# Grouping TensorE matmuls by array shape in a two-layer RWKV-7 and latent-attention step

## The chip, the cores and the metric

The kernel runs on one core of one Trainium2 chip. The metric is the device time of one execution in microseconds (us). A change is told from no change by comparing the median of several runs.

## What is computed

One inference step of a two-layer decoder. Layer 0 mixes tokens by an RWKV-7 recurrence; layer 1 is multi-head latent attention over a latent key and value that come from the residual stream after layer 0. 16 meta tokens and 512 prompt tokens go through it, and 8 sequences of 4 new sample tokens each, which see 2048 past tokens in paged caches. Cut to the two parts that matter here, the reference is:

```python
def wkv7_scan(s0, r, decay, k, v, kk, ka):
    def step(s, inp):
        r_t, d_t, k_t, v_t, kk_t, ka_t = inp
        sa = jnp.einsum('bhvk,bhk->bhv', s, kk_t)
        s = s * d_t[:, :, None, :] - sa[..., None] * ka_t[:, :, None, :] + v_t[..., None] * k_t[:, :, None, :]
        return s, jnp.einsum('bhvk,bhk->bhv', s, r_t)
...
def mla_attend(q_lat, q_rope, q_pos, segments):
...
        for lat, kr, kp in segments:
            s = jnp.einsum('bhqr,bkr->bhqk', ql, lat) + jnp.einsum('bhqp,bkp->bhqk', qr, kr)
            s = s.astype(jnp.float32) * ATTN_SCALE
            scores.append(jnp.where(kp[None, None, None, :] <= qp[None, None, :, None], s, -jnp.inf))
        probs = jax.nn.softmax(jnp.concatenate(scores, axis=-1), axis=-1)
```

The state of a head is 64 x 64, there are 16 heads; attention has 8 heads with 128 plain and 64 rotary dimensions.

## The kernel before

**The recurrence.** The 560 tokens are handled in eight chunks of 64 prompt tokens and a ninth with the last 16 prompt tokens and the 32 sample tokens. Heads go in pairs: a pair's two heads lie on partitions 0 to 63 and 64 to 127 (`halves`, index `par`). Two groups of four pairs run one after the other (`chunks(0)`, then `chunks(1)`), and in a group two halves of two pairs each (`hf`) are stepped in turn, so that one's matmuls fill the other's waits. For one half of one chunk, `chunk` (line 898) does: `solve` (two products, L886 and L892, each followed by copies or scalings on ScalarE and VectorE: L888, L893, L894), the product for the new state (L905), whose result VectorE adds to the decayed state (L913, L915), and the **outputs**. For each of its four heads the outputs are two matmuls that add into one 64 x 64 place of a PSUM tile `q`: L920, in which all 128 partitions are summed over (array shape 128 rows x 64 columns), and L921, in which only the head's own 64 partitions are (64 x 64). Nothing in the recurrence waits for the outputs; ScalarE copies them to `Of` (L923). `tail` (line 966 and following) does the same for the ninth chunk, with L1006 and L1007 for eight heads. An fp32 matmul shows in the trace as two records.

Around it, other work is woven in by a table (`PLAN`): the inverses of the chunk matrices (`inverse`, many small steps on VectorE, L637 and L638; `merge`, with 32 x 32 matmuls L839 and L847, whose operands go through DRAM and are loaded by SP, L816 to L824), the late value projections (L326, with transposes L601), and for finished chunks the mixer's output (L1078 to L1096). The second group starts when its inverse and the values are done. The scheduler of the tile layer fixes each engine's order when the program is built.

**The scores.** In `mla`, `scores(h, i)` (line 1583) takes 128 queries of one head against their 144 to 528 keys, in one or two blocks of columns. Each block is a sum of five matmuls (L1594 to L1598); fp32 operands are split in a rounded high part and a low remainder. L1597 multiplies a tile `r`, which has the rotary queries' high part on one half of the partitions and the low part on the other, with `krh`, the high part of the rotary keys, which stands on both halves. L1598 multiplies only the high half of `r` (64 rows) with the low part `krl` of the keys. A last matmul adds the causal mask (L1599). Between the scores TensorE works on the sample tokens' attention over the paged cache (L1678, L1681, L1727), whose pages POOL and SP fetch.

Of the kernel before, what the change touches and what calls it, by code (L numbers as in the profile page):

```python
# [19 lines left out]
D = 1024  # L20
# [34 lines left out]
# ---------------------------------------------------------------- host layout  # L55
# [150 lines left out]
class Kern:  # L206
    NA, NB, NS, NM, NC = 21, 10, 9, 36, 22
# [44 lines left out]
    # ---- tiles  # L252
# [44 lines left out]
    # ---- weights  # L297
# [21 lines left out]
    def mm3(self, v, w, xs, off, n, first=True, last=True):  # L319
        """v: psum [128, 2, n]; w: (hi, lo) [128, kt, 128]; xs: per k-tile (hi, lo)"""  # L320
# [11 lines left out]
    def mmk(self, v, w, xs):  # L332
        """v: psum [128, n]; w: (hi, lo) [128, kt, 128]; xs: per k-tile (hi, lo), n wide"""
        wh, wl = w
        for k, (xh, xl) in enumerate(xs):
            for e, (wt, xt) in enumerate(((wh, xh), (wh, xl), (wl, xh))):
                self.nc.tensor.matmul(v, wt[:, k, :], xt, start=(k == 0 and e == 0), stop=(k == len(xs) - 1 and e == 2))  # L337
# [12 lines left out]
    def low(self):  # L350
        """what follows gives way to what the program has further on"""
# [33 lines left out]
    # ---- setup  # L385
# [23 lines left out]
    # ---- layer 0 mixing  # L409
    def rwkv(self):  # L410
# [23 lines left out]
        # normed input, its shift and the values, in two spans of tokens  # L434
# [134 lines left out]
        # low-rank paths  # L569
# [19 lines left out]
        # receptances; the values leave feature-major and, per chunk, token-major  # L589
# [32 lines left out]
        # inverses of the unit triangular chunk matrices, blocks of 32  # L622
# [47 lines left out]
        # heads in pairs: decay and rate (A), projection (B), chunk operands (C), scores (D)  # L670
# [127 lines left out]
        # recurrence over chunks, two groups of four pairs  # L798
# [98 lines left out]

        def chunk(st, c, hf):
# [19 lines left out]
            for i, pr, par in heads:  # L918
                o = q[halves[par], i * 64:i * 64 + 64]
                nc.tensor.matmul(o, V[:, pr, par, :], W[pr // 2][:, 2 * (pr % 2) + par, 64:128], start=True, stop=False)  # L920
                nc.tensor.matmul(o, Sp[halves[par], i, :], R[halves[par], pr, :], start=False, stop=True)  # L921
# [31 lines left out]
        # the sample tokens against their states, while the pair's operands are here  # L953
# [12 lines left out]
        def tail(st):  # L966
# [36 lines left out]
            for pr, par in heads:  # L1003
                hs = halves[par]
                o = q[hs, pr * 64:pr * 64 + 48]
                nc.tensor.matmul(o, V[:, pr, par, :], W[pr // 2][:, 2 * (pr % 2) + par, 64:112], start=True, stop=False)  # L1006
                nc.tensor.matmul(o, ident[hs, 64 * par:64 * par + 64], RS[hs, pr, 0:48], start=False, stop=True)  # L1007
# [54 lines left out]
        # output of the mixer, two pairs at a time, over columns a..b  # L1062
# [126 lines left out]
        # what is left, woven together: (steps, what must be through, after how many of its steps)  # L1189
# [42 lines left out]
    # ---- what follows an update of a tile of the residual stream  # L1232
    def begin(self, off, names):
        """norm statistics over columns off.. and split inputs with the gains names"""
# [20 lines left out]
    def stat(self, power):  # L1255
        """the mean square of post() to the given power, on all partitions"""
# [15 lines left out]
    def ffn_seg(self, q, a, b):  # L1272
        """a quarter of the hidden units for columns a..b"""
# [96 lines left out]
    # ---- latent attention  # L1370
    def mla(self):
        nc, tc, I, O, x = self.nc, self.tc, self.I, self.O, self.x
        ident = self.k["ident"]
        mp = self.mp
        mk = mp.tile([128, 320], BF16, name="mk")
# [52 lines left out]
        # down projections  # L1428
# [42 lines left out]
        # queries  # L1471
# [31 lines left out]
        # sample queries against the latent  # L1503
# [24 lines left out]
        # keys and values of the prompt, two heads at a time  # L1528
        KB = [(0, 16)] + [(16 + 128 * i, 128) for i in range(4)]
        kn, V, oo = [], [], [None] * NH  # L1530
        kh, kl = self.a("krh", dt=F32R), self.a("krl", dt=F32R)
        self.split(kh[:, :TP], kl[:, :TP], kr[:, :TP])
        zero = self.c("zero", [128, 512])
        nc.gpsimd.memset(zero, 0.0)
# [367 lines left out]
```

## Time and profile before

| | |
|---|---|
| median of 3 runs | 1768.58 us (1764.98 to 1772.23) |
| profiled execution, span from first to last instruction (the page gives no other time of it) | 1768.4 us |
| TensorE matmuls (PE) | 1653.7 us, 94% of the span |
| VectorE (DVE) | 970.6 us, 55% |
| ScalarE (ACT) | 665.8 us, 38% |
| GpSimd (POOL) | 349.0 us, 20% |
| mean granted TensorE clock | 0.937 |

Matmuls are pipelined, and the page models their ends, so busy shares of PE are no measure of how well it is used. What one matmul costs in a stream is read from the times at which neighbours start. The granted clock of a stretch is a mean: 1.00 is all of it at 2.4 GHz, 0.50 all of it at 1.2 GHz.

### The profile page before, as it was taken

The page shows a single profiled execution, that of the slowest core. Times are in us where ns is not written, and L with a number is a line of the kernel's source. Part 1 is how long each engine was busy: PE and PEld are TensorE (multiplying, and loading weights), DVE is VectorE, ACT ScalarE, POOL GpSimd, SP SyncE. Part 2 cuts the span into 40 slices and gives each one's busy share as a digit, 9 for nine tenths or more (in the row PEclk, how much of TensorE's full clock was granted, in tenths as well). Part 3 has the DMA queues.
Part 4 walks back from the last instruction along what each step waited for, and adds up shares of the span by engine and source line. Part 5 has one row for each costly group of instructions (what it writes and reads, how often), then busy time and mean ns, then how long its engine had stood idle before and what let it go on. Part 6 is the DMA issues. An engine that isn't in the chain of part 4 may idle for free.

```text
span 1768.4 us, 33338 instructions
## 1 busy us (share of the span) xinstructions
PE 1653.7 (94%) x13474; PEld 1494.1 (84%) x13474; DVE 970.6 (55%) x1600; ACT 665.8 (38%) x1232; POOL 349.0 (20%) x467
## 2 busy tenths in 40 slices
PE   7788878899999998899999999899999999999997
PEld 6577867777779887799999999766769999999996
DVE  6775696553426658665444565645635444444446
ACT  4374554322324433334333243244624332322222
POOL 4633435421100023200000010674420000000000
PEclk9899887796669999999999999999999999999999
DMA  6335647855623444444323243587622222322233
GB/s 211 111 101 150 189 145 202 254 173 133 191 92 100 156 157 154 144 153 148 113 85 97 84 134 106 174 254 230 211 85 92 86 86 84 93 87 84 86 93 99
DMA packets 156475, 240.04 MB, mean 136 GB/s; under 512 B 68417, under 2 KB 100082, under 8 KB 156322
## 3 DMA queue, kind: packets, MB, share of 16 engines
q1 hardware_dynamic: 140466, 189.59, 35.5%
q0 software_dynamic: 15280, 47.59, 8.3%
q8 instruction: 106, 1.74, 0.4%
q10 hardware_dynamic: 576, 0.74, 0.1%
q14 instruction: 47, 0.39, 0.1%
HBM read 200.50 MB, written 37.37 MB: 135 GB/s over the span
## 4 chain that ended last, share of the span: by engine, by line
PE 53%; ACT 1%; DVE 1%; issue 1%; DMA 1%; SPq 1%; POOL 0%; DVEq 0%; POOLq 0%; ACTq 0%
PE mm L326 30%; PE mm L337 12%; PE sm L337 2%; PE sm L1727 2%; PE sm L1634 1%; PE sm L1678 1%; PE mm L1598 1%; PE sm L1579 1%; PE sm L1618 1%; PE mm L1594 1%; ACT whi L307 0%; PE sm L1681 0%; DVE y L1839 0%; DVE wlo L308 0%; DMA lN<-latN,idx 0%
## 5 line engine op out<-in xcount | busy, mean ns | idle before, releaser
L307 ACT CAST whi<-raw 128x1024 fp32r<-128x1024 f32 x218 | 228.9, 1050 | 642.9 <-PE mm L326 357.9
L308 DVE TENSOR_TENSOR wlo<-raw,whi 128x1024 fp32r<-128x1024 f32 x214 | 266.7, 1247 | 279.2 <-ACT whi L307 276.9
L337 PE MATMUL mm<-xs,whi 128*128 128x256 f32 (+1 forms) x1024 | 200.7, 294 | 1.7 <-DVE fd L1299 0.9
L337 PEld LDWEIGHTS mm<-xs,whi 128*128 128x128 f32 x1024 | 163.3, 189 | 3.2 <-issue 1.4
L337 PE MATMUL mm<-xs,wlo 128*128 128x256 f32 (+1 forms) x512 | 149.7, 292 | 0.8 <-DVE wlo L308 0.8
L326 PE MATMUL mm<-hh,whi 128*128 128x272 f32 (+1 forms) x640 | 133.6, 290 | 0.0
L326 PE MATMUL mm<-hl,whi 128*128 128x272 f32 (+1 forms) x640 | 133.5, 290 | 0.0
L326 PE MATMUL mm<-hh,wlo 128*128 128x272 f32 (+1 forms) x640 | 133.5, 290 | 0.0
L326 PE MATMUL mm<-h_ffn,whi 128*128 128x272 f32 x512 | 106.2, 288 | 0.5 <-ACT fr L1333 0.5
L326 PE MATMUL mm<-h_ffn,wlo 128*128 128x272 f32 x512 | 106.3, 289 | 0.0
L326 PE MATMUL mm<-l_ffn,whi 128*128 128x272 f32 x512 | 105.8, 288 | 0.0
L326 PEld LDWEIGHTS mm<-hh,whi 128*128 128x128 f32 x640 | 100.9, 188 | 0.0
L326 PEld LDWEIGHTS mm<-hl,whi 128*128 128x128 f32 x640 | 100.9, 188 | 0.0
L326 PEld LDWEIGHTS mm<-hh,wlo 128*128 128x128 f32 x640 | 100.9, 189 | 0.0
L337 PEld LDWEIGHTS mm<-xs,wlo 128*128 128x128 f32 x512 | 96.8, 189 | 1.1 <-DVE wlo L308 1.0
L1837 POOL TENSOR_TENSOR y<-x,rstd 128x272 f32<-128x272 f32 x4 | 3.5, 891 | 459.5 <-ACT rstd L1831 459.5
L337 PE MATMUL mm<-hh,wlo 128*128 128x256 f32 (+1 forms) x256 | 77.0, 301 | 5.1 <-DVE wlo L308 5.1
L326 PEld LDWEIGHTS mm<-h_ffn,whi 128*128 128x128 f32 x512 | 80.8, 188 | 1.0 <-ACT fr L1333 1.0
L326 PEld LDWEIGHTS mm<-l_ffn,whi 128*128 128x128 f32 x512 | 80.3, 188 | 0.0
L326 PEld LDWEIGHTS mm<-h_ffn,wlo 128*128 128x128 f32 x512 | 80.0, 188 | 0.0
L337 PE MATMUL mm<-hl,whi 128*128 128x256 f32 (+1 forms) x256 | 76.7, 300 | 3.1 <-DVE hl L1291 3.0
L337 PE MATMUL mm<-hh,whi 128*128 128x256 f32 (+1 forms) x256 | 77.4, 302 | 0.1
(471 smaller groups left out, 3953.8 us busy)
## 6 DMA issues: line engine op xcount, KB each, us to landing
raw<-wall SPq DMA_DIRECT2D x222, 512.0 KB, 3.6
lT<-latT SPq DMA_DIRECT2D x80, 160.0 KB, 3.5
W_D<-sc POOLq DMA_DIRECT2D x16, 512.0 KB, 4.3
W<-W_D SPq DMA_DIRECT2D x32, 256.0 KB, 3.9
AK_D<-akt SPq DMA_DIRECT2D x8, 576.0 KB, 4.4
s<-state SPq DMA_DIRECT2D x16, 256.0 KB, 3.8
AKc<-AK_D SPq DMA_DIRECT2D x16, 256.0 KB, 4.0
V_D<-vt POOLq DMA_DIRECT2D x8, 288.0 KB, 3.5
```

Source lines behind the costliest of these rows:

```text
L307: nc.scalar.copy(hi, raw)
L308: self.lo_on.tensor_sub(lo, raw, hi.bitcast(F32))
L326: nc.tensor.matmul(v[:, h, :], wt[:, k, :], xt[:, off + h * n: off + (h + 1) * n], start=(first and k == 0 and e == 0), stop=(last and k = ...
L337: self.nc.tensor.matmul(v, wt[:, k, :], xt, start=(k == 0 and e == 0), stop=(k == len(xs) - 1 and e == 2))
L1579: nc.tensor.matmul(o, l[:, k0:k0 + kw], w[:, 2 + k, :], start=(k == 0 and e == 0), stop=(k == 1 and e == 2))
L1594: nc.tensor.matmul(o, qh[:, qs], nh[:, ks], start=True, stop=False)
L1598: nc.tensor.matmul(o, r[b, qs], kl[b, ks], start=False, stop=x < nb - 1)
L1618: nc.tensor.transpose(q[:, 128 * b:128 * b + 128], Pt[:, 16 + 128 * b:144 + 128 * b], ident)
L1634: nc.tensor.matmul(q[:, q0:], V[h // 2][b][:, 128 * (h % 2):128 * (h % 2) + 128], PT[b] if b else Pm[h % 2], start=(b == 0), stop=(b == 4))
L1678: nc.tensor.matmul(q[32 * bb:32 * bb + 32, cols], qlT[:, r, 4 * g + bb, :], lt[bb][:, :, 128 * r + 64 * k:128 * r + 64 * k + 64], start=(r ...
L1727: nc.tensor.matmul(qa[rs, 0:RANK], PT[jp // 2][:, o:o + 32], nat[bb][:, RANK * k:RANK * k + RANK], start=(jp == 0 and k == 0), stop=False)
L1837: nc.gpsimd.tensor_mul(y[:, i], x[m][:, s], r)
```

## The change

In `chunk` and `tail` the two output terms no longer alternate head by head. A helper takes the pairs in turn: for an even pair both heads' first term and then both heads' second, for an odd pair the other way round, so that neighbouring pairs meet in the same shape. In `mla` the low part of the rotary keys becomes two tiles of 128 rows, one with the keys on the upper half and zeros on the lower, one the other way; the fifth matmul of a score takes all 128 rows of `r`.

```diff
-    NA, NB, NS, NM, NC = 21, 10, 9, 36, 22
+    NA, NB, NS, NM, NC = 21, 10, 9, 37, 22
...
+        def alternate(inner, outer, prs):
+
+            for i, pr in enumerate(prs):
+                first, second = (outer, inner) if i % 2 else (inner, outer)
+                first(i, pr, True)
+                second(i, pr, False)
...
             q = self.sm()
-            for i, pr, par in heads:
-                o = q[halves[par], i * 64:i * 64 + 64]
-                nc.tensor.matmul(o, V[:, pr, par, :], W[pr // 2][:, 2 * (pr % 2) + par, 64:128], start=True, stop=False)
-                nc.tensor.matmul(o, Sp[halves[par], i, :], R[halves[par], pr, :], start=False, stop=True)
+
+            def inner(i, pr, first):
+                for par in range(2):
+                    nc.tensor.matmul(q[halves[par], i * 64:i * 64 + 64], V[:, pr, par, :], W[pr // 2][:, 2 * (pr % 2) + par, 64:128], start=first, stop=not first)
+
+            def outer(i, pr, first):
+                for par in range(2):
+                    nc.tensor.matmul(q[halves[par], i * 64:i * 64 + 64], Sp[halves[par], i, :], R[halves[par], pr, :], start=first, stop=not first)
+            alternate(inner, outer, [2 * hf, 2 * hf + 1])
...
-        kh, kl = self.a("krh", dt=F32R), self.a("krl", dt=F32R)
-        self.split(kh[:, :TP], kl[:, :TP], kr[:, :TP])
         zero = self.c("zero", [128, 512])
         nc.gpsimd.memset(zero, 0.0)
+        kh = self.a("krh", dt=F32R)
+        nc.scalar.copy(kh[:, :TP], kr[:, :TP])
+        kz = [self.a(f"krl{i}", dt=F32R) for i in range(2)]
+        for i, (a, b) in enumerate((halves, halves[::-1])):
+            nc.vector.tensor_sub(kz[i][a, :TP], kr[a, :TP], kh[a, :TP].bitcast(F32))
+            for c in (slice(0, TP // 2), slice(TP // 2, TP)):
+                nc.scalar.copy(kz[i][b, c], zero[b, :TP // 2])
...
-                nc.tensor.matmul(o, r[b, qs], kl[b, ks], start=False, stop=x < nb - 1)
+                nc.tensor.matmul(o, r[:, qs], kz[h % 2][:, ks], start=False, stop=x < nb - 1)
```

`tail` is changed like `chunk`, over `range(4)` pairs. In the built programs the orders of TensorE stand as follows.

TensorE in the recurrence of the first group, chunk 4, before: the end of a half's state product (`SUV`, `AKc`), its outputs, the rest of the other half's product, and the start of that half's outputs.

```order
L905 MATMUL sm<-SUV_4_3764,AKc_4_3765 64x64 x5
L920 MATMUL sm<-W_40_3762,SUV_4_3764 64x64
L921 MATMUL sm<-R_4_3766,Sp 64x64
L920 MATMUL sm<-W_40_3762,SUV_4_3764 64x64
L921 MATMUL sm<-R_4_3766,Sp 64x64
```

The same place in the change, both halves' outputs (L912, L928 and L932 are what L905, L920 and L921 were):

```order
L912 MATMUL sm<-SUV_4_3764,AKc_4_3765 64x64 x5
L928 MATMUL sm<-W_40_3762,SUV_4_3764 64x64 x2
L932 MATMUL sm<-R_4_3766,Sp 64x64 x4
L928 MATMUL sm<-W_40_3762,SUV_4_3764 64x64 x2
L912 MATMUL sm<-SUV_4_3764,AKc_4_3765 64x64 x3
L928 MATMUL sm<-W_41_3763,SUV_4_3764 64x64 x2
L932 MATMUL sm<-R_4_3766,Sp 64x64 x4
L928 MATMUL sm<-W_41_3763,SUV_4_3764 64x64 x2
```

Before, the pattern of two rows goes on to eight matmuls; now the same eight stand in three runs, and the run of the second term is four long. Over the whole program, neighbouring matmuls of different array shape number 733 before and 455 after.

ScalarE ahead of the first head's keys, in the change (`krl` are the two padded tiles, `knh` the first head's keys):

```order
L1552 CAST krh<-kr 128x528
L1557 CAST krl_11435<-zero 64x264 x2
L1557 CAST krl_11436<-zero 64x264 x2
L1561 CAST Vm_11443<-zero 80x256
L1561 CAST Vm_11444<-zero 80x256
L1561 CAST Pm_11445<-zero 80x512
L1561 CAST Pm_11446<-zero 80x512
L1572 CAST knh<-mm 128x528
```

The four casts of `krl` are new in this queue; the rest of it is as before. On TensorE the attention's scores and the sample's matmuls also change places in a few stretches. SP's queue moves in two places and POOL's in none.

## Rows read from the trace of the kernel before

**Rows 1.** The page, parts 1 and 2: busy time by engine, granted clock by slice.
```profile
PE 1653.7 (94%) x13474; PEld 1494.1 (84%) x13474; DVE 970.6 (55%) x1600; ACT 665.8 (38%) x1232; POOL 349.0 (20%) x467
...
PEclk9899887796669999999999999999999999999999
```

**Rows 2.** TensorE's waits from 345 to 535 us: total, times, longest.
```profile
PE mm L1085 <- ACT sqo L1081: 1.8, 1, 1.8
```

**Rows 3.** Windows, line 921 alone: PE and weight-load busy (records), clock, DMA share, GB/s.
```profile
345.00:394.00 49.00, 9.75 (x60) 5.63 (x60) 1.00 0.67 194
394.00:447.00 53.00, 13.74 (x68) 8.15 (x68) 0.60 0.48 128
447.00:490.00 43.00, 12.05 (x64) 7.09 (x64) 0.70 0.73 211
490.00:536.00 46.00, 9.28 (x49) 5.49 (x48) 0.71 0.26 78
560.00:590.00 30.00, 2.60 (x16) 1.50 (x16) 1.00 0.43 137
```

**Rows 4.** Timeline of TensorE from 353.9 us, high clock: start, length, line, shape, records.
```profile
353.97 0.69 PE L905 MATMUL sm<-SUV,AKc 128*64 128x64 f32 x16
354.49 0.28 PE L920 MATMUL sm<-W,SUV 128*64 128x64 f32 x2
...
356.49 0.40 PE L326 MATMUL mm<-xvl,whi 128*128 128x280 f32 x1
```

**Rows 5.** Timeline of TensorE, low clock: one call's outputs, first row and next work.
```profile
473.70 0.42 PE L920 MATMUL sm<-W,SUV 128*64 128x64 f32 x2
...
476.88 0.58 PE L905 MATMUL sm<-SUV,AKc 128*64 128x64 f32 x5
```

**Rows 6.** Timeline of TensorE, low clock: two runs in one shape.
```profile
470.67 1.12 PE L886 MATMUL sm<-SUV,W 128*64 128x64 f32 x16
471.79 1.12 PE L892 MATMUL sm<-rb,TT 64*64 64x64 f32 x16
```

**Rows 7.** Timeline of TensorE, high clock: a score with 400 keys.
```profile
1180.53 0.35 PE L1596 MATMUL mm<-knl,qnh 128*128 128x400 f32 x1
1180.72 0.34 PE L1597 MATMUL mm<-krh,qrs 128*128 128x400 f32 x1
1180.99 0.44 PE L1598 MATMUL mm<-krl,qrs 64*128 64x400 f32 x1
1181.37 0.23 PE L1599 MATMUL mm<-mk 128*128 128x128 bf16 x1
```

**Rows 8.** Timeline of ScalarE: the first casts from the zero tile.
```profile
1134.83 0.71 ACT L1538 CAST Vm<-zero 80x256 fp32r<-80x256 f32 x2 [8.64 <-POOL zero L1534]
```

**Rows 9.** Windows: busy PE, PEld, DVE, ACT, POOL (instructions), clock, DMA share, GB/s.
```profile
345.00:372.00 27.00, 27.00 (x265) 23.05 (x263) 22.90 (x64) 7.82 (x22) 9.45 (x14) 1.00 0.65 183
460.00:470.00 10.00, 9.78 (x111) 7.44 (x110) 5.37 (x17) 3.47 (x12) 1.67 (x4) 0.97 0.91 264
470.00:480.00 10.00, 10.00 (x83) 7.68 (x84) 1.74 (x6) 2.15 (x8) 0.85 (x3) 0.50 0.67 207
536.00:619.00 83.00, 81.39 (x650) 74.21 (x648) 53.43 (x96) 37.41 (x64) 8.16 (x16) 1.00 0.42 131
```

**Rows 10.** Timeline of SP's queue: the second group's inverse, first and last issues.
```profile
421.83 0.38 SPq L640 DMA_DIRECT2D X_D<-X  x1
...
430.25 8.50 SPq L824 DMA_DIRECT2D TT<-X_D  x14
```

**Rows 11.** DMA issues from 345 to 535 us: that load, KB each, us to landing.
```profile
TT<-X_D SPq DMA_DIRECT2D x16, 32.0 KB, 2.2
```

**Rows 12.** Timeline of TensorE: the last run that uses it.
```profile
443.73 1.91 PE L847 MATMUL sm<-TT,zs 32*32 32x32 f32 x62 [0.30 <-ACT zs L842]
```

**Rows 13.** Timeline of POOL: the second of twenty page gathers in a row.
```profile
1274.45 0.95 POOL L1720 DMA_INDIRECT lN<-latN,idx  x1 [0.30 <-issue]
```

**Rows 14.** Timeline of VectorE: the first half's next input.
```profile
473.93 0.61 DVE L913 TENSOR_TENSOR SUV<-sm,SL 64x128 f32<-64x128 f32 x2 [4.43 <-issue]
```

More of the change, by code (lines that the diff above doesn't have):

```diff
@@ L1002, in tail, with inner, outer @@
             q = self.sm()
[L1003 to L1007, printed above, removed]
+            def inner(i, pr, first):
+                for par in range(2):
+                    nc.tensor.matmul(q[halves[par], pr * 64:pr * 64 + 48], V[:, pr, par, :], W[pr // 2][:, 2 * (pr % 2) + par, 64:112], start=first, stop=not first)
+            def outer(i, pr, first):
+                for par in range(2):
+                    hs = halves[par]
+                    nc.tensor.matmul(q[hs, pr * 64:pr * 64 + 48], ident[hs, 64 * par:64 * par + 64], RS[hs, pr, 0:48], start=first, stop=not first)
+            alternate(inner, outer, range(4))
             for i in range(2):
@@ L1374, in mla @@
         mp = self.mp
+        halves = (slice(0, 64), slice(64, 128))
         mk = mp.tile([128, 320], BF16, name="mk")
@@ L1583, in scores @@
         def scores(h, i):
-            a, b = (slice(0, 128), slice(0, 64)) if h % 2 == 0 else (slice(0, 128), slice(64, 128))
             n = 16 + 128 * (i + 1)
```

## The prediction, made before the change was run

> **What bounds the kernel now.** I read the page first: TensorE (PE) is busy for 94% of the span, and the clock it was granted is at its high level except in a few slices early in the program [rows 1]. Those slices hold the recurrence over chunks, so I took the list of waits there next: in 190 us the longest line of TensorE's waits is 1.8 us [rows 2]. The time there is therefore TensorE's own, and the question is what it does with it. The two lines that the change rearranges run at 345 to 536 us and again at 577 to 590 us [rows 3]; 257 records of L921 were found, two to a matmul and eight to a call of `chunk`, so 32 calls. The granted clock of these windows is 1.00, 0.60, 0.70, 0.71 and 1.00. Of its two levels (1.2 and 2.4 GHz) a mean of 0.60 means a fifth of the time at the high one, so the records divide into 60 + 14 + 26 + 21 + 16 = 137 at the high level (53%) and 120 at the low one.
>
> The timeline shows where the time goes in one call. At the high level eight matmuls that alternate between 128x64 and 64x64 last from 354.49 to 356.49 us, 0.25 us each; just before, eight matmuls of L905, all 128x64, took 353.97 to 354.49, 0.065 each [rows 4]. At the low level the alternating eight last from 473.70 to 476.88, 0.40 us each [rows 5], and eight of L886 in one shape at most 1.12, of which 0.3 is the last one's own length and the wait for the copy behind it: about 0.11 each [rows 6]. **One change of shape thus costs about 0.185 us at the high level and 0.29 at the low one**, 0.234 as a mean over the 53 and 47 per cent.
>
> **The change, part by part.** In the built programs, neighbouring matmuls of different shape number 733 before and 455 after, 278 fewer.
>
> 1. Chunk outputs. Inside a call seven changes become two (5 x 32 = 160), and 18 calls more now end in the shape of what follows them, so 178 go. 178 x 0.234 = **41.7 us** of TensorE's time. Nothing else in the recurrence moves: the other engines' rows stand as they did, but for a few rows of VectorE's inverse.
> 2. Tails. Two calls of `tail`, together 20 changes fewer, one at each level: 10 x 0.29 + 10 x 0.185 = **4.7 us**.
> 3. Scores. With 400 keys, the matmul before the 64-row one starts 0.19 us after its neighbour, the 64-row one 0.27 after that, and the next 0.38 later [rows 7]. Three full-height ones would take 0.19 each: 0.08 + 0.19 = 0.27 us, and 40 such matmuls give **10.8 us**. A padded matmul streams the same columns, so it costs no more than its full-height neighbours.
> 4. What is added. Four ScalarE casts of zeros and one more VectorE subtract. ScalarE's zero casts before were two in 0.71 us and began when POOL's memset was done [rows 8]; four more stand behind the same memset and ahead of the first head's keys, which come 1.4 us later at most. The subtract falls where VectorE waits for TensorE anyway. The sample's scores cover it on TensorE; without them all of it would show. I charge 1 us (bounds 0 and 1.5).
>
> That is 57.2 - 1 = 56 us of TensorE's time at unchanged clocks. Not all of it can reach the end:
>
> - In the first chunks VectorE is busy 22.9 of 27 us [rows 9], so three calls gain little there: -2 (bounds 0 and -3.5).
> - The second group's recurrence needs its inverse, which goes through DRAM: SP issues those transfers almost without a break from 421.83 to 430.25 + 8.50 = 438.75 us [rows 10]. TensorE, which now has some 6.4 us less to do in that stretch (four calls at 1.6), will stand and wait for them. The last piece lands 2.2 us after 438.75 and is used at 443.73 [rows 11, 12], so there are 2.8 us of slack, and the rest is lost: -4 (bounds 0 and -6.4).
> - In attention POOL issues page gathers back to back at 1.25 us each, twenty in a row, 25 us [rows 13]; faster scores there only wait longer for pages: -4 (bounds 0 and -8).
>
> What comes back is clock. From 460 to 470 us, with 111 records, TensorE had 0.97; from 470 to 480, with 83 records of the same lines, 0.50 [rows 9]. The change draws the records together, so some low stretches should rise. By the clock column [rows 3] 53 x 0.8 + 43 x 0.6 + 46 x 0.58 = 95 us are at the low level; some 20 belong to the merge of the inverse, whose own records stay as they are, and 15 calls lose 1.7 us each, which leaves 49. If half of these rise, and three quarters of that is TensorE's own time, 24 x 0.75 / 2 = 9 us go. This is the term I know least: bounds 0 and 18, and I take +9, since the row with 111 records is as near to the new density as the one with 83.
>
> Sum: 56 - 2 - 4 - 4 + 9 = 55 us. The profiled execution's span is 1768.4 us, and the median of the runs, 1768.58, is the same to 0.2 us, so **1713 us**.
>
> One rule speaks against term 1. The four 64x64 matmuls that now stand together use both row halves of the array and write one bank. L892 does the same today: sixteen records of 64x64, both halves, one bank, and they take 1.12 us as L886's sixteen do [rows 6], which have full height. The Trainium skill, TensorEngine Tiling (Array Packing), "Gotcha 1: PSUM Pressure", says that different row tiles cannot access the same PSUM bank at once; by that rule the halves would take turns and a run of four would cost double. The row shows no such turn, so the sum goes by the row; the other result is rival C.
>
> **The rivals.**
>
> A. *The recurrence itself becomes the bound.* A chunk's chain runs solve, copy, solve, two scalings, product, two additions. At the low level a round's first matmul starts at 470.67 [rows 6], and VectorE has the first half's next input at 473.93 + 0.61 = 474.54 [rows 14]: 3.9 us, where TensorE's work of a round will be three runs of sixteen records at 1.12 and two calls of outputs at 1.4, 6.2 us at the low level, and 3 x 0.52 + 2 x 0.8 and some waits, near 4 us, at the high one. So the chain should be near to binding, and not quite there. If it binds in half of the rounds, 20 of term 1's 42 us and of the clock term are lost: 1735 us. For it: ScalarE and VectorE do nothing faster. Against: the two halves of a group overlap.
>
> B. *The high clock holds through nearly all of the recurrence.* Then the clock term is 18 instead of 9, and part of what SP's issue keeps back comes later in the span: 1703 us, or a few less.
>
> C. *Row halves take turns on a bank.* Four matmuls per call at twice 0.065 or 0.11: +0.26 or +0.44, times 32, some 11 us back: 1724 us. (That is the time by the rule cited above.)
>
> D. *The gap is not the change of shape* but two matmuls adding into the same place of the bank, or an alternation of operands. Then term 1 and 2 vanish, and the kernel takes about 1763 us, no measurable change. Against it: in the scores all of one block's matmuls add into the same place, and only the 64-row one has gaps before and behind it [rows 7].
>
> E. *The clock falls where it is high now*, and the kernel is slower. Fewer busy microseconds could be read as less activity. Between 345 and 394 us and between 536 and 619 us [rows 3, 9] 132 us are at the high level; with three quarters of it TensorE's own time, a microsecond of it at the low level adds 0.75. It decides from 85 us on (64 us: the 55 gained and the 9 that a measurement needs); with all of it the time is 1713 + 99 = 1812 us. For it: only the thin stretches are low now. Against it: the change makes thin stretches denser, and the wide matmuls keep their clock today next to the same thin ones.
>
> **How the numbers follow.** Forecast 0.62, A 0.12, B 0.14, C 0.05, D 0.04, E 0.03. A measurement of this kernel can tell about 0.5%, 9 us, from no change; so faster has 0.93 (the forecast, A, B, C), same 0.04 (D), slower 0.03 (E). The forecast's own bounds, 0 to 18 for the clock and the three losses at their ends (0 and 18 together), reach from 1694 to 1730; with B and A inside, the range is 1691 to 1739, which leaves out D, E and the edges, under 2 in 10.
>
> **What would show it.** Right: records of the first output line in pairs beside runs of eight of the second, two long gaps per call and not seven; a call of 0.8 us at the high level and 1.4 at the low (2.0 and 3.2 now); the score's fifth matmul 0.19 us behind the fourth; the first rows of the merge (L839) no longer straight behind a chunk's outputs but after a pause of some microseconds; a higher granted clock from 394 to 520 us. The prediction is wrong in its mechanism if the two lines' runs still show 0.25 us per matmul, and wrong in its sum if TensorE's idle time in the recurrence grows by more than 10 us (A), or if the gain of the two windows before and after 447 us together is under 30 us.

## The result, and the profile after

The changed kernel takes **1706.77 us** (median of 4 runs, 1704.49 to 1711.19) beside 1767.99 us (4 runs, 1764.98 to 1772.23) of the kernel before: ratio 0.9669, 95% interval 0.9636 to 0.9701. The forecast was 1713 us in a range of 1691 to 1739. The profiled execution spans 1703.3 us at a mean clock of 0.952 (1768.4 and 0.937 before). Runs over 1.5% above the fastest of their kernel count as slow and are left out of the ratios here and below, not of the medians.

The page's parts 1 and 2 of the changed kernel, which answer to [rows 1]:

```profile
PE 1575.3 (92%) x13474; PEld 1442.5 (85%) x13474; DVE 972.1 (57%) x1601; ACT 667.0 (39%) x1236; POOL 348.4 (20%) x467
...
PEclk9889897698899998999999999999999999999998
```

The number of matmuls is the same (13474), their busy time is 78 us shorter, and the clock's row has lost most of its dip in the recurrence: slices 10 to 12 of the 40 were 6, 6, 6 and are 8, 8, 9. The 7 and the 6 that are left stand in slices 7 and 8, ahead of the first chunk; these were low before too, so not all of the low slices held the recurrence, as the prediction read them. Where the 65.1 us between the two spans came from shows in the windows of four stretches that begin and end at the same work: the first chunk's solve, the first row of the merge, the first state product of the sample tokens, their first scores, the first product with the value weights. The kernel before:

```profile
346.00:435.00 89.00, 88.66 (x820) 69.58 (x818) 46.61 (x147) 22.27 (x68) 21.98 (x43) 0.83 0.60 170
435.00:578.00 143.00, 139.42 (x1326) 113.52 (x1327) 64.44 (x163) 52.28 (x134) 14.46 (x33) 0.77 0.44 127
578.00:1130.00 552.00, 531.62 (x3975) 511.14 (x3978) 318.94 (x398) 201.65 (x278) 58.34 (x73) 0.99 0.41 129
1130.00:1315.00 185.00, 174.00 (x1714) 120.08 (x1707) 96.61 (x280) 83.08 (x245) 97.78 (x105) 0.98 0.67 205
```

And the changed kernel (columns as in [rows 9]: stretch, length, busy time and instructions of PE, PEld, DVE, ACT and POOL, clock, DMA share, GB/s):

```profile
347.70:413.00 65.30, 59.04 (x824) 48.90 (x824) 48.54 (x147) 22.26 (x69) 22.49 (x43) 1.00 0.80 226
413.00:526.00 113.00, 103.47 (x1327) 87.78 (x1327) 64.01 (x163) 51.98 (x133) 14.40 (x33) 0.90 0.58 164
526.00:1072.00 546.00, 525.45 (x3967) 506.53 (x3970) 319.42 (x398) 201.37 (x278) 58.84 (x73) 0.99 0.41 131
1072.00:1253.00 181.00, 166.81 (x1720) 119.94 (x1714) 98.08 (x281) 84.73 (x249) 96.83 (x105) 0.96 0.68 210
```

The reader should subtract them line by line. The recurrence gives 24 + 30 = 54 us, the stretch with the tails 6, attention 4, and what lies behind it 3; 1.7 are lost ahead of the first chunk. In the recurrence TensorE's busy time falls by 30 + 36 = 66 us, so its idle time **grows by 12**: it was 0.3 + 3.6 and is 6.3 + 9.5. The clock goes from 0.83 to 1.00 and from 0.77 to 0.90.

TensorE's timeline of one call of `chunk` at the high clock (start, length, engine, line, operation, tiles, shape, records), beside [rows 4]; L928 and L932 are the two output terms:

```profile
356.24 0.29 PE L928 MATMUL sm<-W,SUV 128*64 128x64 f32 x4
356.45 0.45 PE L932 MATMUL sm<-R,Sp 64*64 64x64 f32 x8
356.83 0.34 PE L928 MATMUL sm<-W,SUV 128*64 128x64 f32 x4
357.10 0.40 PE L326 MATMUL mm<-xvl,whi 128*128 128x280 f32 x1
...
455.65 0.69 PE L932 MATMUL sm<-R,Sp 64*64 64x64 f32 x8
456.27 0.48 PE L928 MATMUL sm<-W,SUV 128*64 128x64 f32 x4
456.54 0.72 PE L886 MATMUL sm<-SUV,W 128*64 128x64 f32 x10
```

The call lasts from 356.24 to 357.10, 0.86 us where it was 2.0. Its eight records of 64x64 take 0.38 us together, with the change of shape at their end. The last three lines are of a call at the low clock: its last twelve records take 0.89 us, so all sixteen some 1.2, where it was 3.2 [rows 5].

A score with 400 keys in the changed kernel, beside [rows 7]: the padded fifth matmul starts 0.18 us behind the fourth, as the others do behind their neighbours.

```profile
1118.68 0.34 PE L1618 MATMUL mm<-knl,qnh 128*128 128x400 f32 x1
1118.87 0.34 PE L1619 MATMUL mm<-krh,qrs 128*128 128x400 f32 x1
1119.05 0.35 PE L1620 MATMUL mm<-krl,qrs 128*128 128x400 f32 x1
```

What TensorE waits for in the recurrence now, in the changed kernel's list of waits (total, times, longest), where the longest line was 1.8 us [rows 2]:

```profile
PE sm L839 <- DMA xt<-XT_D: 4.2, 1, 4.2
PE mm L1102 <- ACT sqo L1098: 3.2, 1, 3.2
PE mm L1113 <- DMA lg<-lorag: 2.0, 1, 2.0
PE sm L892 <- ACT rb L888: 1.2, 6, 0.3
PE sm L847 <- DMA TT<-X_D: 1.1, 2, 0.7
PE sm L912 <- DVE SUV L893: 1.0, 3, 0.7
```

The merge now stands and waits for its loads, 4.2 and 1.1 us. The mixer's output, which is woven in, waits for ScalarE (L1102) and for a load (L1113), 5.2 us together. The two-step solve of a chunk waits for ScalarE and VectorE (L888, L893), as a chain does, but for only 2.2 us in all. And the rounds of the second group, by the timeline of its first solve product:

```profile
440.41 0.64 PE L886 MATMUL sm<-SUV,W 128*64 128x64 f32 x16
...
444.50 0.64 PE L886 MATMUL sm<-SUV,W 128*64 128x64 f32 x16
```

A round takes 4.1 us at the high clock. The prediction's figures for it were 3 x 0.52 + 2 x 0.8, 3.2 us and some waits, for TensorE, and 3.9 for the chain alone (read at the low clock).

### The profile page after: what moved, and what is told of

Same layout as the page of the kernel before. It is cut to its first block, busy times and chain, and to the rows that moved or that the text cites. A ratio compares the mean times of both kernels' runs of the same rounds, so it can differ in the third digit from the quotient of the medians.

```text
span 1703.3 us, 33334 instructions
## 1 busy us (share of the span) xinstructions
PE 1575.3 (92%) x13474; PEld 1442.5 (85%) x13474; DVE 972.1 (57%) x1601; ACT 667.0 (39%) x1236; POOL 348.4 (20%) x467
## 4 chain that ended last, share of the span: by engine, by line
PE 54%; DVE 2%; ACT 2%; DMA 1%; issue 1%; SPq 1%; POOL 0%; DVEq 0%; ACTq 0%; POOLq 0%
PE mm L326 31%; PE mm L337 12%; PE sm L337 2%; PE sm L1749 2%; PE sm L1656 1%; PE sm L1700 1%; ACT whi L307 1%; PE sm L1602 1%; DMA lN<-latN,idx 1%; PE sm L1640 0%; DVE wlo L308 0%; PE sm L1703 0%; DMA raw<-wall 0%; DVE y L1861 0%; PE mm L1616 0%
## 5 line engine op out<-in xcount | busy, mean ns | idle before, releaser
L307 ACT CAST whi<-raw 128x1024 fp32r<-128x1024 f32 x218 | 228.8, 1050 | 639.7 <-PE mm L326 356.9
L308 DVE TENSOR_TENSOR wlo<-raw,whi 128x1024 fp32r<-128x1024 f32 x214 | 267.4, 1250 | 280.1 <-ACT whi L307 278.2
L326 PE MATMUL mm<-hh,wlo 128*128 128x272 f32 (+1 forms) x640 | 133.5, 290 | 0.0
L326 PE MATMUL mm<-hl,whi 128*128 128x272 f32 (+1 forms) x640 | 133.4, 290 | 0.0
L326 PE MATMUL mm<-hh,whi 128*128 128x272 f32 (+1 forms) x640 | 133.3, 290 | 0.0
L326 PE MATMUL mm<-h_ffn,whi 128*128 128x272 f32 x512 | 106.2, 289 | 0.5 <-ACT fr L1350 0.5
L326 PE MATMUL mm<-l_ffn,whi 128*128 128x272 f32 x512 | 105.8, 288 | 0.0
L326 PE MATMUL mm<-h_ffn,wlo 128*128 128x272 f32 x512 | 105.4, 287 | 0.0
L326 PEld LDWEIGHTS mm<-hh,whi 128*128 128x128 f32 x640 | 101.1, 188 | 0.0
L326 PEld LDWEIGHTS mm<-hh,wlo 128*128 128x128 f32 x640 | 100.9, 188 | 0.0
L326 PEld LDWEIGHTS mm<-hl,whi 128*128 128x128 f32 x640 | 100.7, 188 | 0.0
L326 PEld LDWEIGHTS mm<-h_ffn,whi 128*128 128x128 f32 x512 | 79.9, 188 | 1.0 <-ACT fr L1350 1.0
L326 PEld LDWEIGHTS mm<-l_ffn,whi 128*128 128x128 f32 x512 | 80.2, 188 | 0.0
L326 PEld LDWEIGHTS mm<-h_ffn,wlo 128*128 128x128 f32 x512 | 80.1, 188 | 0.0
```

The source lines that it names most:

```text
L307: nc.scalar.copy(hi, raw)
L308: self.lo_on.tensor_sub(lo, raw, hi.bitcast(F32))
L326: nc.tensor.matmul(v[:, h, :], wt[:, k, :], xt[:, off + h * n: off + (h + 1) * n], start=(first and k == 0 and e == 0), stop=(last and k = ...
```

## The experiments

The questions, in order: is the price really the change of shape (and not two adds into one place, rival D, or row halves that take turns, rival C); what each part is worth; what sets the pace in the recurrence now; what the clock does; and where the scores' gain goes. They ran in three sessions on three chips, each beside the kernel before, whose medians there were 1805.96 us (chip A, 23 runs), 1762.35 (chip B, 11 runs) and 1758.2 (chip C, 11 runs), so times are compared inside a session only.

One thing has to be read first. The kernel before varies from run to run by 18 to 25 us (22, 9 and 11 runs that count in the ratios), and nearly all of that follows its mean granted clock: on chip C 1767.41 us at 0.934, 1760.85 at 0.938, 1754.57 at 0.947, 1749.01 at 0.949. A line through a session's runs falls by 1229, 1274 and 1174 us per unit of clock on chips A, B and C (correlations -0.94, -0.96 and -0.98). "At equal clock" below means a run's distance from that line, as a mean over the runs; for kernels with a higher clock than any run of the kernel before the line is drawn on beyond its runs.

### The outputs alone (chip A)

`chunk` and `tail` as in the change, `mla` as before.

```diff
-            for i, pr, par in heads:
...
+            alternate(inner, outer, [2 * hf, 2 * hf + 1])
```

> Only the outputs of chunk and tail are grouped by shape; the scores are as before. The parts of the gain are additive by my theory: the recurrence ended 54 us earlier in the changed kernel and the start of attention 58, so 1768 - 57 = 1711 us (1706 to 1716). If the padded keys carried a larger part (by making the attention's order better), the time is 1720 or more.

Measured: 1750.18 us (4 runs), ratio 0.9701 (0.965 to 0.9751), 42 us under the kernel before at equal clock and with the clock itself up to 0.944 as a mean. By the ratio that is 1715 of 1768 us, inside the range expected. The windows of the recurrence:

```profile
344.00:407.50 63.50, 58.41 (x820) 48.30 (x820) 48.30 (x147) 22.27 (x69) 22.83 (x43) 0.99 0.79 231
407.50:523.70 116.20, 104.99 (x1319) 88.61 (x1320) 63.46 (x162) 51.54 (x133) 14.36 (x33) 0.87 0.54 160
```

The two stretches take 179.7 us, as in the changed kernel (178) and not as before (232, above). So the whole gain of the recurrence belongs to the outputs, as term 1 had it.

### The scores alone (chip A)

`mla` as in the change, `chunk` and `tail` as before.

> Only the low rotary keys are padded; the outputs alternate as before. By the theory that a change of shape costs 0.08 + 0.19 us around each of 40 matmuls, 11 us of TensorE's time go, and POOL's page gathers keep some of it back: 1768 - 6 = 1762 us (1757 to 1765). If the gathers and the page transfers set the pace of attention, it is 1768; if all of it shows, 1757.

Measured: 1798.88 us (12 runs), ratio 0.995 (0.9917 to 0.9984). Its mean clock was 0.932, about that of the kernel before (0.933); at equal clock it is 11 us faster, by the medians 7. That is about the 10.8 of term 3, with little or nothing taken off. On chip C the same edit was worth much less on top of the outputs (below).

### Seven changes of shape, but of other places (chip A)

The changed kernel, with the eight matmuls of a call again alternating in shape, in an order in which a term seldom follows the other term of its own head: five of the seven changes go to another place of the bank.

```diff
-            alternate(inner, outer, [2 * hf, 2 * hf + 1])
+            for j, k in enumerate((0, 1, 1, 0, 2, 3, 3, 2)):
+                term(j % 2, k, j % 4 < 2)
```

> The changed kernel, with the eight matmuls of a chunk's outputs in an order in which the shape changes at every one of the seven steps, as before, but only two of the seven steps (four before) add into the place that the matmul ahead wrote. If the change of shape is the cost, the gain of the chunk outputs goes: 1768 - 6 (scores) - 5 (tails) = 1757 us (1750 to 1762), and every step shows about 0.15 us at the high clock whether the place is the same or another. If adding into one place is the cost, half of the outputs' gain stays: about 1732 us, and only steps within one place are long.

Measured: 1789.36 us (10 runs), ratio 0.992 (0.988 to 0.996); at equal clock 16 us under the kernel before, 5 more than the scores alone give. The tails, which are grouped here, were forecast at 4.7, so the crossed chunks give nothing. The timeline of TensorE, where L932 is the 128x64 term here and L930 the 64x64 one:

```profile
351.48 0.28 PE L932 MATMUL sm<-W,SUV 128*64 128x64 f32 x2
351.69 0.32 PE L930 MATMUL sm<-R,Sp 64*64 64x64 f32 x2
351.94 0.33 PE L932 MATMUL sm<-W,SUV 128*64 128x64 f32 x2
352.20 0.33 PE L930 MATMUL sm<-R,Sp 64*64 64x64 f32 x2
```

From 351.69 to 351.94 both matmuls add into the same place, from 351.94 to 352.20 into two: 0.25 and 0.26 us, as before the change (about 0.15 was expected of a step). The price does not hang on the place. That it does not hang on the alternation of the two terms' operands either is shown by the padded kernel below, in which they alternate in one shape at no cost. So it hangs on the change of shape, and rival D falls.

### No outputs at all (chip A)

The changed kernel without the second half of `chunk`: both output terms and the copies of them are left out (the output tiles are filled with a constant), so TensorE has the least to do in the recurrence.

```diff
...
-            alternate(inner, outer, [2 * hf, 2 * hf + 1])
-            o = 64 * (c % 4)
-            nc.scalar.copy(Of[p0, TA * (c // 4)][:, :, o:o + 64], pk(q, 2))
...
+                        nc.gpsimd.memset(t, 0.5)
```

> The changed kernel without the two output terms of the chunks and without their copies (the mixer's output of the 512 prompt tokens is computed from a constant instead); the recurrence, the tails and all else stay. What it tells: whether TensorE or the chain of the recurrence sets the pace after the change. If TensorE still does, 32 calls of 0.85 us go: 1707 - 25 = 1682 us (1676 to 1690). If the chain does, a round of two halves, now 4.1 us, keeps about 3.5 of them and little goes: 1697 to 1706. If the thinner stream also lets the clock fall to its low level in the recurrence, it is 1706 or more, and the granted clock of that stretch shows it.

Measured: 1757.94 us (4 runs), ratio 0.9737 (0.9687 to 0.9788). It is **slower than the outputs alone**, which do more. The windows from the first solve to the merge and from there to the first state product of the sample tokens:

```profile
346.30:416.00 69.70, 56.48 (x561) 45.30 (x561) 46.41 (x147) 18.41 (x53) 21.32 (x38) 0.84 0.71 208
416.00:532.00 116.00, 104.56 (x1183) 87.52 (x1183) 66.21 (x171) 51.56 (x130) 17.93 (x41) 0.87 0.55 158
```

Together they take 186 us, 6 more than with the outputs. In the first 70 us TensorE was idle for 13, its clock was 0.84 instead of 0.99, and its 561 records were busy nearly as long as the 820 of the kernel with outputs. Its longest wait there is now the chain's own: 5.9 us for the next chunk's input from VectorE. Over the four runs the mean clock is 0.936, where the outputs alone had 0.944; by the line above that is worth 10 us, more than the 8 that were lost. Less work came with a lower clock, so this kernel alone can't tell the chain's time from TensorE's.

### The changed kernel again, without a change of shape, and with a filler (chip B)

Three kernels of one session. The changed kernel as it is:

> The changed kernel as it is, on the chip of the three runs beside it, so that these can be read against it. A ratio to the kernel before of 0.965 to 0.970; runs within 6 us of each other, where those of the kernel before spread over 20 to 27 us with their mean granted clock.

The changed kernel with the second term padded to 128 rows, as the scores were (`R` holds each head's operand with zeros on the other half), so that a call has one shape throughout:

```diff
...
-nc.tensor.matmul(q[halves[par], i * 64:i * 64 + 64], Sp[halves[par], i, :], R[halves[par], pr, :], start=first, stop=not first)
+nc.tensor.matmul(q[halves[par], i * 64:i * 64 + 64], Sp[:, i, :], R[:, pr, par, :], start=first, stop=not first)
```

> The changed kernel with the second output term of the chunks padded too: the chunk's receptance tile has zeros on the other head's partitions, so that all eight matmuls of a call are 128x64 and no change of shape is left inside a call (one more load by SP, two small memsets on POOL per chunk). If TensorE still sets the pace of the recurrence, 64 changes of 0.12 us over a plain step and the better start of two runs go: 8 to 10 us below the changed kernel beside it. If the chain of the recurrence or SP's loads set it, within 3 us of it; slower by more than 3 us if SP's additional loads (16 of some 0.4 us) are in the way.

And the kernel without outputs, with one wide matmul of constants per call in their place, to keep TensorE's clock up with less work:

```diff
...
+            q = self.sm()
+            nc.tensor.matmul(q[0:64, 0:256], ident[:, 0:64], cst["d0"][:, 0:256], start=True, stop=True)
```

> The kernel without the chunks' outputs (the mixer's output of the 512 prompt tokens is left to a constant), but with one matmul of 256 columns of constants, 128x64, in place of each call's eight: 0.2 us of TensorE's time in place of 0.8, with about as many columns. Without outputs the granted clock in the recurrence fell (22 of 70 us low before the merge, none in the changed kernel). If that fall is why leaving out 26 us of work gained nothing, the filler keeps the clock and the time is 10 to 20 us below the changed kernel beside it. If the chain sets the pace even at the high clock, it is within 6 us of the changed kernel.

Measured: 1703.13 us (ratio 0.9688, 0.9624 to 0.9752), 1707.6 (0.97, 0.9635 to 0.9764) and 1704.52 (0.9696, 0.9633 to 0.9759), four runs each: no difference that can be told. The recurrence's windows of the changed kernel, of the padded one and of the one with the filler, in three fences:

```profile
344.00:407.50 63.50, 58.60 (x822) 48.48 (x821) 48.59 (x147) 22.29 (x69) 21.94 (x43) 0.99 0.79 231
407.50:522.40 114.90, 105.09 (x1321) 88.88 (x1322) 63.86 (x163) 51.88 (x133) 14.75 (x33) 0.87 0.55 162
```

```profile
349.00:415.50 66.50, 55.65 (x817) 47.51 (x817) 45.78 (x149) 22.56 (x69) 24.84 (x52) 0.97 0.74 217
415.50:526.70 111.20, 102.66 (x1319) 87.53 (x1320) 64.58 (x160) 51.36 (x133) 17.04 (x41) 0.90 0.60 168
```

```profile
349.00:416.80 67.80, 54.52 (x594) 43.07 (x592) 45.82 (x147) 18.24 (x53) 21.93 (x38) 0.96 0.70 212
416.80:528.00 111.20, 100.30 (x1124) 83.27 (x1125) 62.47 (x160) 47.60 (x117) 15.49 (x35) 0.90 0.56 161
```

TensorE is busy for 163.7, 158.3 and 154.8 us of them, and the stretch takes 178.4, 177.7 and 179.0: 5 and 9 us less work give nothing. **Over the whole recurrence TensorE no longer sets the pace.** The parts differ, in one trace of each kernel: with less work the first stretch is 3.0 and 4.3 us longer, and the second 3.7 shorter in both, which is within the 111 to 115 us that this stretch takes in the kernels with the same outputs. By the lists of waits, several things set the pace in turn: the merge's load (2.8, 4.4 and 6.7 us in the three kernels), the mixer's output, which waits for ScalarE and for a load (5.5, 3.3 and 6.6), the chain through ScalarE and VectorE, and a chunk's own loads (with the filler one solve waited 1.0 us for `SUV` from DRAM). VectorE is busy for 9.2 and 9.7 of the first two 10 us of the changed kernel's first profile, but TensorE has no idle time there. No run parts these from each other. The padded kernel also gives the price of a change a second time, by its timeline at the high clock (L933 and L937 are the two terms, two calls one behind the other):

```profile
359.91 0.29 PE L933 MATMUL sm<-W,SUV 128*64 128x64 f32 x4
360.02 0.40 PE L937 MATMUL sm<-R,Sp 128*64 128x64 f32 x8
360.26 0.40 PE L933 MATMUL sm<-W,SUV 128*64 128x64 f32 x8
360.49 0.40 PE L937 MATMUL sm<-R,Sp 128*64 128x64 f32 x8
360.72 0.29 PE L933 MATMUL sm<-W,SUV 128*64 128x64 f32 x4
```

A call of one shape takes 0.46 us (half of the 0.81 from the first to the last start and the 0.11 of four records). The alternating call, 2.0 us up to the next work, has eight changes and not seven, since the 128x128 matmul behind it (L326) has another shape too: (2.0 - 0.46) / 8 = 0.19 us each. In the grouped call the step to L326 is also a change, so its 0.86 us hold three: 0.13 each. From the call's first row to the first L928 behind its L932 there are two changes and 0.59 us; the padded call takes 0.35 for the same twelve records, so these two cost 0.12 each. The changes that are left are thus cheaper than those that went: five fewer saved 1.14 us, 0.23 for each.

### The merge's loads on two queues (chip B)

The changed kernel, with half of the loads behind the merge issued by ScalarE instead of SP, since SP still issues for 17 us there.

```diff
-nc.sync.dma_start(ts[i][o + 32 * b:o + 32 * b + 32, :, bs], X_D[st][b, o // 64, i].rearrange("c s t -> s c t"))
+(nc.scalar if b else nc.sync).dma_start(ts[i][o + 32 * b:o + 32 * b + 32, :, bs], X_D[st][b, o // 64, i].rearrange("c s t -> s c t"))
```

> The changed kernel, with half of the 16 loads of the second group's inverse (TT from X_D) issued by ScalarE's queue. In the changed kernel SP issues for this merge from 404.2 to 421.2 us while TensorE pauses. If SP's issue is what holds the second group up there, 8 issues of 0.49 us go from it: about 4 us below the changed kernel beside it. If the values' way through DRAM (V_D) holds it up, which ends at about the same time, within 1 us of it.

Measured: 1701.31 us (6 runs, 1697.05 to 1709.16), ratio 0.9686 (0.9637 to 0.9735), beside the changed kernel's 1703.13: not to be told apart. SP's issue of these loads costs at most a few us. In the trace TensorE's wait for `TT` is gone (1.3 us in the changed kernel beside it), but its pause ahead of the merge is for another load, `xt`, which stayed on SP: 3.8 us here and 2.8 there. What else keeps the second group (that load, or the values' way through DRAM) was not tried.

### Where the scores' gain goes (chip C)

Three kernels: the changed one, the one with the outputs alone, and the changed one without the fifth matmul of each score.

> The changed kernel again, on the chip of the next three, as their base. 1703 us at a clock of 0.95, as in the two earlier sessions (1706.8 and 1703.1), or as much above it as the kernel before is above 1765 on this chip.

> Outputs of chunks and tails grouped, scores as before: what the scores' term is worth with the clock already at 0.95. By the sum of the prediction (10.8 for the matmuls, 1 for the casts, 4 for the pages) 6 us over the changed kernel; by the stretch from the sample's first scores to the value products, which became 4.4 us shorter, 4 us over it, or 7 with the 3 that were won behind it. No difference at all would say that TensorE does not set the pace in attention.

```diff
-                nc.tensor.matmul(o, r[:, qs], kh[:, ks], start=False, stop=False)
-                nc.tensor.matmul(o, r[:, qs], kz[h % 2][:, ks], start=False, stop=x < nb - 1)
+                nc.tensor.matmul(o, r[:, qs], kh[:, ks], start=False, stop=x < nb - 1)
```

> The changed kernel without the fifth matmul of each score (the rotary queries with the low part of the rotary keys is left out of the scores; the padded tiles are still made). 40 matmuls at 0.12 to 0.19 us, 6.4 us. If TensorE sets the pace in attention, 6 us under the changed kernel; if the page gathers do, as the prediction's loss of 4 us supposes, at most 2 us under it.

Measured (6 runs each): 1703.99 us (ratio 0.9688, 0.9651 to 0.9725), 1707.06 (0.9712, 0.9675 to 0.9748) and 1701.32 (0.9679, 0.9639 to 0.9719). The medians differ by 3.1 and 2.7 us, within the spread of 9 to 15 us, so the traces have to say it. The windows from the sample's first scores to the value products, of the outputs alone, of the changed kernel and of the one without the fifth matmul:

```profile
1069.00:1252.40 183.40, 173.71 (x1722) 120.84 (x1721) 98.65 (x281) 83.07 (x245) 96.60 (x106) 0.97 0.66 207
```

```profile
1070.90:1249.70 178.80, 164.40 (x1723) 118.04 (x1722) 97.79 (x281) 85.14 (x249) 97.11 (x106) 0.99 0.68 212
```

```profile
1067.30:1246.50 179.20, 163.65 (x1681) 115.09 (x1681) 98.50 (x281) 83.27 (x249) 94.93 (x106) 0.97 0.68 212
```

With the padded keys TensorE is busy for 9.3 us less, and its idle time grows from 9.7 to 14.4, so 4.6 are left. Without the fifth matmul at all the stretch is no shorter in these traces, so TensorE doesn't set its pace there either. (Over the runs, at equal clock, the three are 38, 40 and 44 us under the kernel before, with an uncertainty of 1 us or more each; some 4 us between the last two are in the runs that these traces don't show.) The wait that takes the rest is in the chain of waits of the changed kernel's first profile (start, length, what):

```profile
1179.19 6.41 DMA raw<-wall
1185.62 1.05 ACT whi L307
1186.70 1.22 DVE wlo L308
1187.92 0.61 DVE ol L375
1188.58 1.20 PE sm L1700 x14
```

A weight load lands at 1185.6. ScalarE's rounding of it (L307) and VectorE's remainder (L308) wait for it, an unrelated split (L375) stands behind them in VectorE's queue, and the sample's scores (L1700) wait for that, 3.2 us in this kernel's list of waits. In the kernel with the outputs alone ScalarE had to wait 0.15 us for the same load, by its timeline:

```profile
1182.86 1.05 ACT L307 CAST whi<-raw 128x1024 fp32r<-128x1024 f32 x1 [0.15 <-DMA raw<-wall]
```

and its TensorE shows no such wait. With faster scores the splits reach the load before the load is there. The kernel without the fifth matmul meets the same load, and TensorE then waits 4.9 us for a ScalarE copy that stands behind this cast:

```profile
1183.75 1.04 ACT L307 CAST whi<-raw 128x1024 fp32r<-128x1024 f32 x1 [6.37 <-DMA raw<-wall]
```

That the load is the whole cause is argued from these waits; no run moved it earlier.

### A filler in the kernel before (chip C)

The kernel before, with the same wide matmul of constants behind each call's outputs: would it lift the clock there as well?

> The kernel before, with one 128x64 matmul of 256 columns of a constant added behind each call's outputs (not part of the computation): 32 of them at some 0.42 us with the high clock, 0.84 with the low one. If thin alternating matmuls are what lowers the clock, and denser ones raise it, the mean clock goes from 0.938 to 0.95 or more with a narrow spread, and the 13.5 us added are nearly paid back: about the time of the kernel before. If the clock stays as it is, some 20 us over the kernel before, with its spread.

Measured: 1794.08 us (6 runs), ratio 1.0213 (1.0169 to 1.0257), at a mean clock of 0.937, where the kernel before had 0.943 on this chip. Of the two cases expected the second came, with its size wrong: the clock did not rise, and the time rose by 36 us and not 20; at equal clock it is 32. The windows, beside those of the kernel before above:

```profile
346.00:421.60 75.60, 73.14 (x725) 57.39 (x723) 46.05 (x138) 20.33 (x61) 18.49 (x33) 0.95 0.59 178
421.60:583.40 161.80, 154.75 (x1375) 119.94 (x1376) 62.99 (x161) 50.49 (x131) 14.31 (x35) 0.78 0.39 116
```

The first stretch has 0.95 (0.83 before), the second 0.78 (0.77 before). But the edit adds a step to each call, which moved other woven work (820 records became 725 in the first stretch), so the kernel tells little of the clock; it shows that these wide matmuls, put in for the clock's sake, did not pay.

## Why the prediction was right, and where it was not

The time fell 6 us under the forecast, well inside the range, and the mechanism forecast is the one that was measured. In its number the result lies nearer to rival B (1703 us), and of the prediction's three signs of being wrong one came: TensorE's idle time in the recurrence grew by more than 10 us, so its sum was wrong in its parts. That the total came out close is in part luck, since the errors nearly cancelled.

- **The price of a change of shape held.** 0.185 us was forecast at the high clock, and the alternating call against the padded one gives 0.19. A call of 0.8 us was to be seen and 0.86 was; 1.4 at the low clock, and some 1.2. The crossed order and the padded kernel show that it is the change of shape and not the place or the operands that cost.
- **Term 1 was too small.** It gave each removed change the mean price, but the changes that stay became cheaper too: a call lost 1.14 us at the high level and 2.0 at the low one. By the prediction's own split, 17 and 15 of 32 calls, that is some 49 us, an estimate, where 41.7 was forecast. Term 2 held: the stretch with the tails became 6 us shorter at the same clock of 0.99, and the crossed kernel gives the tails 5 (4.7 forecast). With all losses, and at equal clock, the changed kernel is 44 (chip B) and 40 us (chip C) faster than the one before, where the forecast had 55 - 9 = 46.
- **Term 3 held for TensorE and its loss had the wrong cause.** 9.3 us of busy time went (10.8 - 1 forecast) and 4.7 came back as idle time (4 forecast). But the step "faster scores there only wait longer for pages" failed: waits for pages (the sample's scores on `lT`) rose from 1.7 to 2.4 us between those two kernels, and the new wait, 4.0 us in that trace and 3.2 in the first, was for a weight load on SP, passed on through VectorE's queue. On chip A the scores brought 11 us at equal clock, and the trace there has 1.3 us of this wait; whether that is the whole difference stays open.
- **The losses in the recurrence were too small.** 2 + 4 were taken off; TensorE's idle time grew by 12. For the merge 4 was forecast, and its waits are 4.2 us on `xt` (L839) and 1.1 on `TT`. The 2 that were put down to VectorE in the first chunks don't show: TensorE has no idle time in the first 30 us. The mixer's output, which the prediction gave no loss, waits for 5.2 us where it was 1.8; the chain's steps (L888, L893) wait for 2.2 where it was 0.4; a chunk's own load is 0.8. So the step that failed is the list of what would be late, and not mainly "the chain should be near to binding, and not quite there". The sign is rival A's, but the chain, A's mechanism, is a small part of it in the changed kernel, and A's price of 20 us was too high.
- **The clock term was mis-sized**: +9, with 18 as the upper bound. By the windows some 96 us of the recurrence were at the low level before and 23 are now, and the prediction gave the merge 20, so nearly all of the 49 us rose and not half: that is rival B's case. By the slopes of the runs the rise from 0.937 to 0.952 is worth 18 to 19 us; the mean clocks of the sessions on chips B and C (0.943 to 0.953, 0.943 to 0.955) give 12 and 14. So it was 12 to 19. Term 1 and the clock together were some 10 to 17 us too small, the losses in the recurrence 6, and these errors had opposite signs. The share is an account and not two separate causes: shorter runs of thin matmuls are also fewer microseconds at the low level.
- **C fell.** Eight 64x64 records in both row halves of one bank take 0.38 us with one change of shape; the padded kernel's eight records of full height take 0.23 to 0.24, and twice that, without any change, would be 0.46 or more. The rule of the Trainium skill behind it, TensorEngine Tiling (Array Packing), "Gotcha 1: PSUM Pressure", does not show here. The same page says under "Key Properties" that changing the tiling mode drains TensorE, without a price; this case agrees in that every change costs time: 0.12 to 0.19 us at the high clock.
- **D and E fell**: by the crossed order and the padded kernel for D, and for E by the clock, which fell in no stretch of the recurrence. In attention it went from 0.98 to 0.96 in the first trace, and was 0.99 on chip C.

## What to carry to other kernels

Count the neighbouring matmuls of different array shape before anything else is moved: in alternation each change cost 0.19 us here at the high clock, three times a thin matmul itself (0.06), and order or zero rows remove it at little cost (a padded fifth matmul of a score starts 0.18 us behind its neighbour, like a full one). Then ask at once what is late next, since 66 us of freed TensorE time in the recurrence gave 54: a load, woven-in work that waits for another engine, a chain between engines, a split at the head of a queue. And where a kernel's time follows its clock from run to run, compare kernels by pairs of time and clock, or a session's luck is taken for an effect.

## What was not expected of the hardware

- TensorE's busy share and its clock don't go together. Before the merge it was busy for 88.7 of 89 us at a clock of 0.83 with alternating thin matmuls, for 59.0 of 65.3 at 1.00 with grouped ones, and for 56.5 of 69.7 at 0.84 without any outputs.
- The kernels that alternate in shape spread more from run to run than those that don't, along with their clock: 25, 24 and 18 us for the kernel before (22, 9 and 11 runs), 27 for the crossed order (10) and 24 for the scores alone (12), beside 4 us for the outputs alone on chip A (4), 7 to 10 for the changed kernel (4, 4 and 6), and 9 to 15 for its variants with six runs. More runs give a wider spread, and the four runs of the kernel before that stand beside the result spread by only 7 us. By standard deviation, which allows for the number of runs, it is 6 to 9 us beside 2 to 5.
- Leaving out all of the outputs made the kernel 8 us slower than keeping them grouped (1757.94 and 1750.18 on one chip), with a clock of 0.84 instead of 0.99 in one stretch.
